# A gated delta mixer: transposed keys copied out of PSUM at once, decays fetched one head ahead

## Chip, cores and metric

The kernel runs on one core of one Trainium2 chip. The metric is the device time of one execution in microseconds. TensorE is written PE, VectorE DVE, ScalarE ACT, GpSimd POOL; SP is the engine whose queue issues the transfers.

## The reference

Two layers act on a sequence of 1024 tokens with 1024 features, all in float32. Each layer is a mixer, a cross-attention over 256 memory rows and a squared-ReLU MLP, each behind an RMS norm and added to the residual. The change lies in the mixer of the second layer, the gated delta rule with 8 heads of 128 x 128. Cut to what matters, it computes:

```
qkv, gate, b, a = split(h @ w_in)
qkv  = silu(short_conv(qkv, conv_w))           # 4 taps along the sequence
q, k = l2norm(q), l2norm(k)                    # per token and head, over 128 features
beta = sigmoid(b);  g = cumsum(-exp(a_log) * softplus(a + dt_bias))   # per chunk and head
decay[t, s] = exp(g[t] - g[s]) for s <= t, else 0
lower = beta * (k k^T) * decay (strict);  attn = (q k^T) * decay
u, w  = solve(1 + lower, [v * beta, k * beta * exp(g)])
per chunk:  v_new = u - w S;  o = (q exp(g)) S + attn v_new
            S = S exp(g_last) + (k exp(g_last - g))^T v_new
out = (rmsnorm(o) * silu(gate)) @ w_out
```

The kernel takes chunks of 128 tokens: eight chunks, four to a half of the sequence.

## The kernel before, in words

Activations are held with features on the 128 partitions and tokens along the free axis, in two halves of 512 tokens. Every large product is done three times with float32 split into a high and a low part (`mm3`). A projection of one head's 128 columns for one half is eight such triples, 24 products of 128x512 into one PSUM bank of tag "mm" (two banks).

`mix_c` runs the mixer. For each pair of heads it calls `gdn_head` twice, then `gdn_inv` (the triangular inverse, through DRAM) and `gdn_rec` (the recurrence over chunks; the last four heads run theirs together). Afterwards come eight gates (`c_gate`), whose projections depend on no head.

`gdn_head` projects keys, queries and values of a head (three weight tiles, both halves) into tiles "raw" (five buffers), and calls `gdn_pre` for each half. `gdn_pre` does this:

- conv and SiLU: one ACT multiply (L1002), three DVE multiply-adds (L1004), a tanh (L1007) and a DVE pass (L1008), for each of the three;
- keys are transposed by PE into a bank of tag "a" called pk (L1014). There are two such banks. ACT squares the four chunks from pk with a running sum (L1017) into `kt`, which serves as scratch here;
- the queries' squares are summed by PE into a second bank pn (L1022), which DVE copies out (L1023). From both sums come the norms, on DVE and with a power on POOL (L1024 to L1033);
- ACT scales the transposed keys, read from pk again, into `kt` (L1031), and `kt` is stored to DRAM;
- the decays M (128x512, the same row for all partitions) are fetched from DRAM into a tile of tag "M" with one buffer (L1037). ACT makes exp(M) for the queries (L1039), POOL multiplies it by the queries and subtracts the mask from M (L1040, L1042), and ACT makes the decay matrices in place (L1045);
- PE multiplies keys with keys and queries, two chunks to a bank of tag "a" (L1050), and DVE multiplies the result by norms and decays into `ua` (L1058), which is stored twice (L1066, L1088). Last, the values are transposed into a bank of tag "a" (L1071) and scaled (L1073).

`c_gate` projects the gate of a head, takes its SiLU (L881, L882), and for the heads 0 to 3 fetches the head's output from DRAM into the tile `e` (L884), multiplies (L885) and stores (L886).

Scratch of 128x512 comes from `tmp()`, tag "T" with five buffers: the conv's accumulators, the squares, the gate's `e`. Weight tiles go through `ldw` (two raw buffers, three split ones). All transfers are issued on SP, whose queue, like each engine's, runs in the order written. That order is fixed when the program is built: a planner goes through the instructions by priority (that of the program's text, unless marked high) and places each where its model of durations and free buffers says that it can start. An instruction whose input or buffer is late on the chip holds all that stand behind it on its engine.

Of the kernel before, what the change touches and what calls it, by code (L numbers as in the profile page):

```python
# [11 lines left out]
F32 = mybir.dt.float32  # L12
F32R = mybir.dt.float32r
BF16 = mybir.dt.bfloat16
AF = mybir.ActivationFunctionType
# [7 lines left out]
HALVES = (0, 1)  # L23
# [3 lines left out]
class Model:  # L27
# [336 lines left out]
    def mix(self, l):  # L364
        if l == 0:
            with self.phase(
                dict(z=3, so=1, ml=2),
                **dict(kq=8, v=4, e=2, sp=2, sh=2, sl=1, wh=2, wl=1, A=2, ah=1, al=1, so_st=1),
            ):
                self.mix_start(l, "so", dict(M=3, W=2, V=2, N=4, C=1, st=1, gg=1, ot=1))  # L370
                self.mix_ab()
                self.out_parts(False)
                self.x_open(self.x_src)
                self.out_proj(self.a["ab_o"])
        else:
            with self.phase(
                dict(a=2, i=1, rec=2, o=1),
                **dict(X=3, Y=2, Uk=1, pr=1, B=4, y=3, S=4, on=2),
            ):
                self.first = [self.ldw(self.a["c_w"][i]) for i in (8, 0)]  # L380
                self.mix_start(l, "o", dict(raw=5, kq=2, vc=1, M=1, qe=1, ua=1, kv=2))
                self.mix_c()
                self.out_parts(True)
                self.x_open(self.x_src, (1,))
                self.out_proj(self.a["c_o"])
# [214 lines left out]
    def ml_heads(self, p):  # L600
        nc = self.nc
        C = None
        for half in HALVES:
# [3 lines left out]
            for i in range(4):  # L607
# [3 lines left out]

                t = self.keep("M", 512, F32)
                qd, k, q = t[:, :256], t[:, 256:384], t[:, 384:]
                t = self.keep("M", 512, F32)
                vT, d = t[:, :256], t[:, 256:]
# [255 lines left out]
    def c_gate(self, h):  # L871

        nc = self.nc

        def gate(i, w, half):
            cols = slice(half * 512, half * 512 + 512)
            t, e = self.stage(), self.tmp()
            ps = self.proj(w, half)
            with self.tc.high_priority():
                self.scaled(t, ps, half)  # L880
            nc.scalar.activation(e, t, AF.Tanh, scale=0.5)  # L881
            nc.vector.scalar_tensor_tensor(out=t, in0=e, scalar=1.0, in1=t, op0=ALU.add, op1=ALU.mult)  # L882
            if h < 4:
                nc.sync.dma_start(out=e, in_=self.od[h][:, cols])  # L884
                nc.vector.tensor_mul(t, t, e)  # L885
            nc.sync.dma_start(out=self.pj[i][:, cols], in_=t)  # L886

        self.lagged([24 + h], lambda i: self.ldw(self.a["c_w"][i]), gate)
# [69 lines left out]
    def gdn_head(self, h):  # L958

        nc = self.nc  # L960
        raw = {}

        def take(i, w, half):
            t = self.ph2("raw", [128, 515])
            ps = self.proj(w, half)
            with self.tc.high_priority():
                self.scaled(t[:, 3:515], ps, half)
                if half == 0:
                    nc.gpsimd.memset(t[:, 0:3], 0.0)
                else:  # L970
                    nc.gpsimd.tensor_copy(t[:, 0:3], raw[i, 0][:, 512:515])
            raw[i, half] = t
            if (i, half) == (16, 0):
                self.c_gates()

        ld = lambda i: self.first.pop(0) if self.first else self.ldw(self.a["c_w"][i])
        self.lagged((8 + h, h, 16 + h), ld, take, 2 if h == 0 else 1)
        oq = self.cols([128, 8])
        for half in HALVES:
            self.gdn_pre(h, half, [raw[i, half] for i in (8 + h, h, 16 + h)], oq)  # L980
        return oq

    def ph2(self, tag, shape):
        pool = self.pr if tag in self.right else self.ph
        return pool.tile(list(shape), F32, tag=tag, name=self.nm(tag), bufs=self.bufs[tag])

    def gdn_pre(self, h, half, raws, oq):

        nc = self.nc
        mm = nc.tensor.matmul
        chunks = [slice(i * 128, i * 128 + 128) for i in range(4)]
        c4 = slice(4 * half, 4 * half + 4)
        kq = self.ph2("kq", [128, 2, 512])
        vc = self.keep("vc", dt=F32)
        for tl, raw, dst in zip((8 + h, h, 16 + h), raws, (kq[:, 0], kq[:, 1], vc)):
            cv = self.tmp()  # L1000
            wj = lambda j: self.convw[:, tl * 4 + j : tl * 4 + j + 1]
            nc.scalar.mul(cv, raw[:, 0:512], wj(0))  # L1002
            for j in range(1, 4):
                nc.vector.scalar_tensor_tensor(  # L1004
                    out=cv, in0=raw[:, j : j + 512], scalar=wj(j), in1=cv, op0=ALU.mult, op1=ALU.add
                )
            nc.scalar.activation(dst, cv, AF.Tanh, scale=0.5)  # L1007
            nc.vector.scalar_tensor_tensor(out=dst, in0=dst, scalar=1.0, in1=cv, op0=ALU.add, op1=ALU.mult)  # L1008
        self.put(h, half, 0, kq[:, 0])

        ss, r, c = (self.small([128, 8]) for _ in range(3))
        pk = self.bank("a")
        for s in chunks:
            nc.tensor.transpose(out=pk[:, s], in_=kq[:, 0, s], identity=self.ident)  # L1014
        kt = self.keep("kv", dt=F32)
        for i, s in enumerate(chunks):
            nc.scalar.activation(kt[:, s], pk[:, s], AF.Square, accum_out=ss[:, i : i + 1])  # L1017
        pn = self.bank("a")
        sq = self.tmp()
        nc.scalar.activation(sq, kq[:, 1], AF.Square)  # L1020
        for i, s in enumerate(chunks):
            mm(pn[:, i : i + 1], sq[:, s], self.ones[:, 0:1], start=True, stop=True)  # L1022
        nc.vector.tensor_copy(ss[:, 4:8], pn[:, 0:4])  # L1023
        nc.vector.tensor_scalar(out=ss, in0=ss, scalar1=0.25, scalar2=EPS, op0=ALU.mult, op1=ALU.add)  # L1024
        nc.gpsimd.tensor_tensor(out=r, in0=ss, in1=self.power, op=ALU.pow)
        nc.vector.reciprocal(c[:, 0:4], ss[:, 0:4])
        nc.vector.tensor_mul(c[:, 0:4], c[:, 0:4], self.gcol("beta", h, half))
        kd = c[:, 4:8]
        nc.vector.tensor_mul(kd, c[:, 0:4], self.gcol("ed", h, half))
        for i, s in enumerate(chunks):  # L1030
            nc.scalar.mul(kt[:, s], pk[:, s], kd[:, i : i + 1])  # L1031
        self.put(h, half, 3, kt)
        nc.vector.tensor_scalar_mul(oq[:, c4], r[:, 4:8], 0.5 * 128.0**-0.5)  # L1033

        M = self.keep("M", dt=F32)
        m3 = M.rearrange("p (c t) -> p c t", c=4)
        nc.sync.dma_start(out=m3, in_=self.gr[c4, h].partition_broadcast(128))  # L1037
        qe = self.keep("qe", dt=F32)
        nc.scalar.activation(qe, M, AF.Exp)  # L1039
        nc.gpsimd.tensor_mul(qe, qe, kq[:, 1])  # L1040
        self.put(h, half, 1, qe)
        nc.gpsimd.tensor_sub(m3, m3, self.mask_a.unsqueeze(1).broadcast_to([128, 4, 128]))  # L1042
        ng = self.gcol("ng", h, half)
        for i in range(4):
            nc.scalar.activation(m3[:, i], m3[:, i], AF.Exp, bias=ng[:, i : i + 1])  # L1045
        ua = self.ph2("ua", [128, 4, 2, 128])
        for i in range(0, 4, 2):
            p = self.bank("a")
            for j in range(2):
                mm(  # L1050
                    p[:, j * 256 : j * 256 + 256].rearrange("p (n t) -> p n t", n=2),
                    kq[:, 0, chunks[i + j]],
                    kq[:, :, chunks[i + j]],
                    start=True,
                    stop=True,
                )
            for j in range(2):
                nc.vector.scalar_tensor_tensor(  # L1058
                    out=ua[:, i + j],
                    in0=p[:, j * 256 : j * 256 + 256].rearrange("p (n t) -> p n t", n=2),  # L1060
                    scalar=c[:, i + j : i + j + 1],
                    in1=m3[:, i + j].unsqueeze(1).broadcast_to([128, 2, 128]),
                    op0=ALU.mult,
                    op1=ALU.mult,
                )
        nc.sync.dma_start(out=self.dense(self.Ud[h])[:, c4], in_=ua[:, :, 0])  # L1066
        self.put(h, half, 2, ua[:, :, 1])

        p = self.bank("a")
        for s in chunks:  # L1070
            nc.tensor.transpose(out=p[:, s], in_=vc[:, s], identity=self.ident)  # L1071
        t = self.keep("kv", dt=F32)
        nc.vector.tensor_mul(  # L1073
            t.rearrange("p (c d) -> p c d", c=4),
            p.rearrange("p (c d) -> p c d", c=4),
            r[:, 0:4].unsqueeze(2).broadcast_to([128, 4, 128]),
        )
        self.put(h, half, 4, t)
# [692 lines left out]
```

## Time and profile before

| | |
|---|---|
| runs | 3222.31, 3226.89, 3231.45 us; median 3226.89 |
| profiled execution | 3224.76 us, its span 3221.8 us |
| mean granted clock of PE | 0.971 of full speed |
| busy share of the span | PE 95%, PE's weight load 78%, DVE 66%, ACT 41%, POOL 29% |
| DMA | 438.04 MB, mean 136 GB/s |
| the chain that ended last | PE 33%, DVE 9%, DMA 4%, issue 4%, POOL 1%, ACT 1% |

The span runs from the first to the last instruction. Shares of busy time are means over stages that differ much. PE's clock has two levels, 1.2 and 2.4 GHz; a granted clock of 0.5 over a stretch means the lower level throughout.

### The profile page before, as it was taken

The numbers are of one execution on the slowest core, as the hardware profiler recorded it, in microseconds if no ns is written. First come the engines' busy times: TensorE is split into PE (matmuls) and PEld (weight loads), VectorE is DVE, ScalarE is ACT, GpSimd is POOL, SyncE is SP. The second block draws the span as 40 slices with busy tenths as digits, with TensorE's granted clock in tenths as the row PEclk, the third lists the DMA queues.
The fourth block names the chain that finished last, engine by engine and source line by source line (L and its number), as shares of the span: only waits on it lengthen the run. The fifth ranks groups of instructions, "written<-read, shape, count | busy, mean of one in ns | idle before, by whom it ended". The sixth has DMA issues, their size and how long they took to land.

```text
span 3221.8 us, 39997 instructions
## 1 busy us (share of the span) xinstructions
PE 3045.2 (95%) x14447; PEld 2511.5 (78%) x14447; DVE 2115.9 (66%) x3342; ACT 1330.2 (41%) x2525; POOL 945.4 (29%) x725
## 2 busy tenths in 40 slices
PE   8999989999899999998988899899999899999997
PEld 6777777888678878887777788788888678878886
DVE  5567475545786667777777775654454786667777
ACT  3254464424354454433443333234333354444442
POOL 2354565313000032234343333125323100023323
PEclk9999989999899999999999899999999999999998
DMA  4333553213244464443345556665212234474432
GB/s 151 109 119 103 156 175 119 70 39 102 75 143 157 152 238 167 147 164 100 87 117 142 149 156 187 191 231 187 66 56 77 97 111 149 157 250 173 148 144 79
DMA packets 268374, 438.04 MB, mean 136 GB/s; under 512 B 38064, under 2 KB 146832, under 8 KB 261008
## 3 DMA queue, kind: packets, MB, share of 16 engines
q1 hardware_dynamic: 268176, 435.50, 41.4%
q8 instruction: 113, 1.85, 0.2%
q14 instruction: 85, 0.70, 0.1%
HBM read 300.60 MB, written 134.81 MB: 135 GB/s over the span
## 4 chain that ended last, share of the span: by engine, by line
PE 33%; DVE 9%; DMA 4%; issue 4%; POOL 1%; ACT 1%; SPq 0%; POOLq 0%; DVEq 0%; ACTq 0%
PE mm L158 3%; PE mm L157 3%; PE mm L156 3%; PE ga L1453 2%; PE ga L1454 2%; PE ga L1455 2%; PE gb L1454 1%; DVE t L1004 1%; PE gb L1455 1%; PE gb L1453 1%; PE gc L1454 1%; PE gc L1455 1%; PE gc L1453 1%; PE mm L1454 1%; PE mm L1455 1%
## 5 line engine op out<-in xcount | busy, mean ns | idle before, releaser
L156 PE MATMUL mm<-hh,wh 128*128 128x512 f32 x1248 | 503.4, 404 | 8.2 <-DVE raw L431 3.5
L157 PE MATMUL mm<-hl,wh 128*128 128x512 f32 x1248 | 504.3, 404 | 0.0
L158 PE MATMUL mm<-hh,wl 128*128 128x512 f32 x1248 | 501.9, 402 | 0.0
L150 POOL TENSOR_TENSOR wl<-wr,wh 128x1024 fp32r<-128x1024 f32 x128 | 320.6, 2506 | 448.8 <-ACT wh L149 423.4
L1445 POOL TENSOR_TENSOR r<-r,r 128x512 f32<-128x512 f32 x64 | 92.0, 1458 | 881.8 <-DVE lo L1412 881.8
L1412 DVE TENSOR_TENSOR lo<-r,hi 128x1024 fp32r<-128x1024 f32 x192 | 252.8, 1317 | 133.1 <-ACT hi L1411 132.3
L1411 ACT CAST hi<-r 128x1024 fp32r<-128x1024 f32 x192 | 201.6, 1051 | 313.7 <-PE mm L1454 126.6
L156 PEld LDWEIGHTS mm<-hh,wh 128*128 128x128 f32 x1248 | 239.4, 192 | 59.2 <-DVE raw L431 4.8
L158 PEld LDWEIGHTS mm<-hh,wl 128*128 128x128 f32 x1248 | 240.5, 193 | 48.3 <-issue 0.9
L157 PEld LDWEIGHTS mm<-hl,wh 128*128 128x128 f32 x1248 | 240.2, 192 | 48.0 <-DVE hl L474 0.4
L149 ACT CAST wh<-wr 128x1024 fp32r<-128x1024 f32 x128 | 133.8, 1046 | 213.2 <-PE mm L157 120.8
L1412 DVE TENSOR_TENSOR lo<-br,hi 128x512 fp32r<-128x512 f32 x224 | 187.0, 852 | 32.9 <-ACT hi L1411 32.8
L1453 PE MATMUL ga<-hi,hi 128*128 128x512 f32 x528 | 206.7, 392 | 1.8 <-ACT w L1550 1.0
L1455 PE MATMUL ga<-hi,lo 128*128 128x512 f32 x528 | 206.5, 391 | 0.0
L1454 PE MATMUL ga<-lo,hi 128*128 128x512 f32 x528 | 206.5, 391 | 0.0
L1411 ACT CAST hi<-br 128x512 fp32r<-128x512 f32 x224 | 133.4, 619 | 152.0 <-PE ga L1455 90.0
L1454 PE MATMUL gb<-lo,hi 128*128 128x512 f32 x432 | 169.8, 393 | 7.6 <-DVE lo L1412 7.6
L1453 PE MATMUL gb<-hi,hi 128*128 128x512 f32 x432 | 169.8, 394 | 3.6 <-ACT hi L1411 3.1
L1454 PE MATMUL gc<-lo,hi 128*128 128x512 f32 x432 | 169.1, 391 | 2.3 <-DVE lo L1412 2.3
L1455 PE MATMUL gb<-hi,lo 128*128 128x512 f32 x432 | 169.0, 392 | 0.0
L1455 PE MATMUL gc<-hi,lo 128*128 128x512 f32 x432 | 168.2, 390 | 0.0
L1453 PE MATMUL gc<-hi,hi 128*128 128x512 f32 x432 | 167.8, 390 | 0.0
(515 smaller groups left out, 7228.5 us busy)
## 6 DMA issues: line engine op xcount, KB each, us to landing
r<-in_w SPq DMA_DIRECT2D x128, 512.0 KB, 4.2
br<-hd SPq DMA_DIRECT2D x56, 1024.0 KB, 5.4
hd<-w SPq DMA_DIRECT2D x160, 256.0 KB, 3.1
B<-Bd SPq DMA_DIRECT2D x64, 384.0 KB, 4.5
hd<-t SPq DMA_DIRECT2D x64, 256.0 KB, 5.2
wr<-in_c_w SPq DMA_DIRECT2D x32, 512.0 KB, 4.3
wr<-in_ab_w SPq DMA_DIRECT2D x24, 512.0 KB, 3.6
pj<-p SPq DMA_DIRECT2D x48, 256.0 KB, 2.1
```

The costliest lines, as they stand in the source:

```text
L149: nc.scalar.copy(hi, raw)
L150: (eng or nc.gpsimd).tensor_sub(lo, raw, hi.bitcast(F32))
L156: mm(out, w[0], x[0], start=first, stop=False)
L157: mm(out, w[0], x[1], start=False, stop=False)
L158: return mm(out, w[1], x[0], start=False, stop=last)
L1004: nc.vector.scalar_tensor_tensor(out=cv, in0=raw[:, j : j + 512], scalar=wj(j), in1=cv, op0=ALU.mult, op1=ALU.add)
L1411: nc.scalar.copy(hi, src)
L1412: (eng or nc.vector).tensor_sub(lo, src, hi.bitcast(F32))
L1445: self.nc.gpsimd.tensor_add(out[:, i : i + 512], a[:, i : i + 512], b[:, i : i + 512])
L1453: mm(ps, hi, b[k][0], start=first and k == 0, stop=False, skip_group_check=True)
L1454: mm(ps, hi, b[k][1], start=False, stop=False, skip_group_check=True)
L1455: mm(ps, lo, b[k][0], start=False, stop=last and k == 3, skip_group_check=True)
```

## The change

The scratch that the squares write is now a tile of its own; the transposed keys are copied to `kt` at once, and squares and scaling read `kt`. The fetch of M moves to a function `decays` that fetches both halves of a head; it is called before the head's projections, or for head 0 behind its gates, which make the rows that it reads. Tag "M" has two buffers in this phase. In the gate the fetch of the head's output goes into a tile `o` of its own, ahead of the projection.

```diff
-                self.mix_start(l, "o", dict(raw=5, kq=2, vc=1, M=1, qe=1, ua=1, kv=2))
+                self.mix_start(l, "o", dict(raw=5, kq=2, vc=1, M=2, qe=1, ua=1, kv=2))
...
             t, e = self.stage(), self.tmp()
+            if h < 4:
+                o = self.tmp()
+                nc.sync.dma_start(out=o, in_=self.od[h][:, cols])
             ps = self.proj(w, half)
...
             if h < 4:
-                nc.sync.dma_start(out=e, in_=self.od[h][:, cols])
-                nc.vector.tensor_mul(t, t, e)
+                nc.vector.tensor_mul(t, t, o)
             nc.sync.dma_start(out=self.pj[i][:, cols], in_=t)
...
         raw = {}
+        if h > 0:
+            M = self.decays(h)
...
         self.lagged((8 + h, h, 16 + h), ld, take, 2 if h == 0 else 1)
+        if h == 0:
+            M = self.decays(h)
         oq = self.cols([128, 8])
         for half in HALVES:
-            self.gdn_pre(h, half, [raw[i, half] for i in (8 + h, h, 16 + h)], oq)
+            self.gdn_pre(h, half, [raw[i, half] for i in (8 + h, h, 16 + h)], oq, M[half])
         return oq
+
+    def decays(self, h):
+
+        tiles = []
+        for half in HALVES:
+            tiles.append(self.keep("M", dt=F32))
+            self.nc.sync.dma_start(
+                out=tiles[half].rearrange("p (c t) -> p c t", c=4),
+                in_=self.gr[4 * half : 4 * half + 4, h].partition_broadcast(128),
+            )
+        return tiles
...
         kt = self.keep("kv", dt=F32)
+        nc.scalar.copy(kt, pk)
+        sq = self.tmp()
         for i, s in enumerate(chunks):
-            nc.scalar.activation(kt[:, s], pk[:, s], AF.Square, accum_out=ss[:, i : i + 1])
+            nc.scalar.activation(sq[:, s], kt[:, s], AF.Square, accum_out=ss[:, i : i + 1])
...
         for i, s in enumerate(chunks):
-            nc.scalar.mul(kt[:, s], pk[:, s], kd[:, i : i + 1])
+            nc.scalar.mul(kt[:, s], kt[:, s], kd[:, i : i + 1])
...
-        M = self.keep("M", dt=F32)
         m3 = M.rearrange("p (c t) -> p c t", c=4)
-        nc.sync.dma_start(out=m3, in_=self.gr[c4, h].partition_broadcast(128))
```

## Rows read from the trace of the kernel before

**Rows 1.** The page: span, and busy time of each engine.

```profile
span 3221.8 us, 39997 instructions
...
PE 3045.2 (95%) x14447; PEld 2511.5 (78%) x14447; DVE 2115.9 (66%) x3342; ACT 1330.2 (41%) x2525; POOL 945.4 (29%) x725
```

**Rows 2.** Windows: stretch, length, PE, PEld, DVE, ACT, POOL busy, clock, DMA share, GB/s.

```profile
1550.00:1730.00 180.00, 163.20 (x740) 131.22 (x738) 150.42 (x267) 76.74 (x200) 69.99 (x59) 0.96 0.41 111
1550.00:2130.00 580.00, 529.17 (x2808) 448.26 (x2807) 415.37 (x847) 210.70 (x560) 181.13 (x145) 0.95 0.53 152
```

**Rows 3.** Groups of PE, 1550:2130: busy, mean ns | idle before, releasers.

```profile
L156 PE MATMUL mm<-hh,wh 128*128 128x512 f32 x466 | 192.9, 414 | 2.8 <-DVE s L1027 2.3 <-DVE raw L431 0.5
...
L1050 PE MATMUL a<-kq 128*128 128x256 f32 x128 | 38.6, 429 | 13.0 <-DVE s L1023 6.6 <-ACT kv L1031 4.5 <-DVE ua L1058 2.0
...
L1071 PE MATMUL a<-ident,vc 128*128 128x128 f32 x64 | 10.5, 284 | 2.8 <-DVE ua L1058 2.8
...
L1014 PE MATMUL a<-ident,kq 128*128 128x128 f32 x64 | 9.8, 273 | 0.9 <-DVE ua L1058 0.9
```

**Rows 4.** Waits, 1540:2130: total us, times, longest.

```profile
ACT qe L1039 <- DMA M<-gr: 101.2, 16, 13.0
...
PE i L1129 <- DMA X<-Xd: 10.2, 4, 3.2
...
DVE p L885 <- DMA t<-od: 7.0, 6, 2.8
...
PE i L1129 <- DMA Uk<-Ud: 2.5, 1, 2.5
```

**Rows 5.** The line that fetches M: issue to landing.

```profile
DMA to landing us min/median/max: 4.7/6.8/8.8
```

**Rows 6.** Order of time, 1704:1717: start, length, instruction, [idle before].

```profile
1704.39 0.72 SPq L1037 DMA_DIRECT2D M<-gr  x1
...
1711.04 0.63 ACT L1039 ACTIVATE qe<-M 128x512 f32<-128x512 f32 x1 [3.43 <-DMA M<-gr]
...
1712.73 0.34 DVE L1024 TENSOR_SCALAR s<-s 128x8 f32<-128x8 f32 x1 [2.90 <-ACT kv L1017]
...
1716.22 0.47 PE L156 MATMUL mm<-hh,wh 128*128 128x512 f32 x1 [2.29 <-DVE s L1027]
```

**Rows 7.** Order of time, 1984:1990.

```profile
1984.52 0.63 ACT L1039 ACTIVATE qe<-M 128x512 f32<-128x512 f32 x1 [5.78 <-DMA M<-gr]
...
1987.01 0.49 PE L1190 MATMUL o<-S,B 128*128 128x128 f32 x2 [1.38 <-ACT on L1192]
...
1988.97 0.49 PE L1180 MATMUL rec<-y,B 128*128 128x128 f32 x2 [1.25 <-DVE y L1177]
```

**Rows 8.** Windows: stretches with a lower clock.

```profile
1595.00:1605.00 10.00, 7.70 (x27) 6.28 (x28) 9.32 (x15) 4.34 (x13) 7.06 (x6) 0.83 0.33 88
...
1715.00:1725.00 10.00, 8.37 (x32) 6.46 (x33) 9.79 (x29) 5.06 (x12) 4.47 (x5) 0.83 0.09 26
...
1985.00:2000.00 15.00, 12.37 (x68) 11.10 (x68) 7.47 (x17) 7.13 (x24) 5.96 (x4) 0.77 0.45 138
...
1730.00:1745.00 15.00, 11.84 (x53) 10.04 (x52) 8.37 (x17) 4.77 (x13) 5.22 (x5) 0.77 0.76 198
...
2085.00:2090.00 5.00, 5.00 (x23) 4.38 (x23) 1.68 (x3) 1.72 (x4) 0.00 (x0) 0.66 0.93 273
```

**Rows 9.** Single lines: min/median/max ns of one.

```profile
L1031 ACT ACTIVATE kv<-a,s x64: 347/367/381, 1575.7 to 1993.5; 128x128 f32<-128x128 f32 x64
...
L1045 ACT ACTIVATE M<-M,gd_ng x64: 384/387/416, 1562.4 to 1989.1; 128x128 f32<-128x128 f32 x64
...
L1550 ACT COPY w<-gb x28: 576/586/593, 896.4 to 2858.2; 128x512 f32<-128x512 f32 x28
```

**Rows 10.** SP's waits, 1540:2130.

```profile
SPq L1066 <- DVE ua L1058: 34.7, 8, 7.5
```

**Rows 11.** Order of time, PE at 2052.

```profile
2052.53 0.49 PE L1171 MATMUL rec<-S,B 128*128 128x128 f32 x2 [1.39 <-DVE S L1185]
```

More of the change, by code (lines that the diff above doesn't have):

```diff
@@ L985, in ph2, with gdn_pre @@
         return pool.tile(list(shape), F32, tag=tag, name=self.nm(tag), bufs=self.bufs[tag])
-    def gdn_pre(self, h, half, raws, oq):
+    def gdn_pre(self, h, half, raws, oq, M):
         nc = self.nc
```

## The prediction, made before the result was known

> **What bounds the kernel now.** I read the page's busy line first, then the second mixer in stretches, then who waits there, and last single stalls in order of time. TensorE (PE) is busy for 95% of the span [rows 1], so a microsecond counts only if PE stands idle in it or runs at a lower clock. The mixer's heads lie between 1550 and 2130 us. There PE is busy 529.17 of 580 us, so 50.8 us are idle, at a mean granted clock of 0.95. In the first 180 us of it VectorE (DVE) is busy 150.42 us, 84%: it is the second limit [rows 2].
>
> Which waits make up the idle time? The largest groups [rows 3]: the products of keys with keys and queries (L1050) wait 13.0 us, all for a bank of tag "a" (6.6 behind DVE's L1023, 4.5 behind ACT's scaling L1031, 2.0 behind L1058); the transposes L1071 and L1014 wait 2.8 and 0.9 us, for the same kind of bank behind L1058; a projection waits 2.3 us behind DVE's L1027; together 19.0 us. The inverse (L1129) waits 10.2 + 2.5 = 12.7 us for round trips through DRAM, and ACT, which is not the bound, waits 101.2 us in 16 waits for the decays M [rows 4]. That load takes 4.7 to 8.8 us to land [rows 5].
>
> That wait reaches PE. At 1704.39 M is issued, behind the stores of the previous half, since its one buffer is read until then. ACT's exponential of M starts at 1711.04 after 3.43 us of waiting, and the squares stand behind it on ACT. So DVE waits 2.90 us for their sum, and PE 2.29 us for a bank that DVE was to empty [rows 6]. The second example is another half: ACT waits 5.78 us for M, and behind it PE stops for 1.38 us (L1190) and 1.25 us (L1180) [rows 7].
>
> After such stops the clock falls. 1595:1605 was granted 0.83, which is 0.17 x 10 = 1.7 us lost. 1645:1650 and 1660:1670 lost 1.7 us each too, and 1715:1725 as well: four stretches, of which the first and the last are shown. 1985:2000, with 0.77, lost 3.45 us [rows 8].
>
> **The change part by part.**
>
> *Keys.* Today bank pk is held from the transposes through the squares, the sums, the power on GpSimd and the scaling L1031. Afterwards one copy frees it. Added are 16 copies of 128x512 out of PSUM; the same form (L1550) takes 586 ns at the median [rows 9], so 16 x 0.586 = 9.4 us of ACT. 128 short ACT operations now read SBUF. L1031 (PSUM, per-partition scale) has a median of 367 ns, L1045 (SBUF, per-partition bias) 387 ns. So 128 x 0.02 = 2.6 us. The other end is no difference, 0; as L1045 is also an exponential, the true price could even be under 0, which I bound by -2.6. I take 2.6, because L1045 is the nearest row with the same size and a scalar operand per partition too. The sum is 12.0 us on ACT, beside the 101.2 us that it waits today. If that cover were gone, ACT's lateness would reach PE at the rate at which it does now: 19.0 us of PE waits (below) against 101.2, or 0.19, so some 2.3 us. The squares also start 0.59 us later per half; this too is shorter than the wait that stood before them.
>
> The row says 20 ns more per short operation. The Trainium skill (Perfetto Trace Analysis, Optimizing Scalar/DVE Operations) speaks against the move: it states an access overhead of some 93 ns for ScalarE on SBUF against 51 ns on PSUM. By it the estimate would be 128 x 0.042 = 5.4 us instead of 2.6, and 14.8 us on ACT; the sum for PE would stay.
>
> What goes on PE: the 4.5 us behind L1031 (the second pair of L1050 needs pk's bank), and part of the 6.6 us behind L1023, since the first pair can take pk's bank instead of the one that L1023 empties. What is late next: both banks are now held by the two pairs until L1058, so L1071 and L1014 still wait for L1058. I therefore keep all waits behind L1058, 2.0 + 2.8 + 0.9 = 5.7 us, as not gained.
>
> *Decays.* The number of loads stays 16. With two buffers the load of a half waits for the same half of the head before, not for the half just done, so it is issued about half a head or more ahead, and a landing of 8.8 us at most is covered by the head's six projections: the row of L156 counts 466 products in the 580 us [rows 2, 3], eight to a projection, so 58 projections, one in 10 us on average. On SP's queue the load moves ahead of the weight loads, of the stores of keys and values, and of the loads of the inverse. All of these stand behind it if its buffer is not free. It waits for L1058, as the store L1066 already does for 34.7 us in 8 waits, at most 7.5 [rows 10]. A load that is queued after that store adds nothing; one queued before it holds weights for up to 7.5 us, which two weights in hand (three buffers, two projections each) cover. Only head 0 loads behind its own gates, as before. GpSimd's two passes over M move earlier but stay the same.
>
> *Gate.* For four heads the eight loads of earlier outputs go out before the projection, into a tile of their own. No load is added, but each holds one of the five "T" tiles through a projection. DVE waits 7.0 us for these loads today, in 6 waits [rows 4]; behind one of them PE stops 1.39 us at 2052.53 [rows 11]. I count 1.4. Bounds: 0 (the tile comes free late) and all of 7.0.
>
> *The sum.* PE waits 13.0 + 2.8 + 0.9 + 2.3 = 19.0 around the banks, 2.6 behind M at 1987 to 1989 [rows 7], 1.4 at the gate, and clock 4 x 1.7 + 3.45 = 10.25: together 33.3 us. Less the 5.7 behind L1058: 27.6 us. I count half. The order on each engine is fixed by a planner from modelled times, so the new order will have other places where PE comes too early; the profile can't show them, and half lies midway between "all gone" and "all replaced". That gives -13.8 us. The profiled execution took 3224.8 us (3221.8 of span and 3.0 around it), so 3211.0; the median of the three runs is 2.1 us above it: 3213 us.
>
> **The rivals.**
>
> 1. *Given back* (no change). M is no longer late, but PE's next limits are near: DVE at 84%, and the waits behind L1058. If only the 4.5 us behind L1031 and one clock fall of 1.7 go, the time is 3221. For it: DVE's load does not change by one instruction. Against it: DVE itself waits for ACT, as the 2.90 us show. That the change doesn't do what it says, because the loads are still issued late on SP, ends here too.
>
> 2. *All of it* (faster). Every counted stall goes, the ones behind L1058 as well, because M and the sums are both early: 3226.9 - 33.3 = 3194. For it: the waits in [rows 6, 7] have one root. Against it: with two banks of tag "a" something always waits for the second.
>
> 3. *The inverse comes out* (slower). The inverse's stores and loads through DRAM are covered by the work that PE does meanwhile. If the preparation of the heads runs through sooner, that work is used up sooner, and PE stands at L1129 more often. Five times today it waits there, 12.7 us in all [rows 4], and the stretches after have clocks of 0.77 (15 us), 0.66 (10), 0.66 (5), 0.66 (10) and 0.66 (5), of which the first and the last are shown [rows 8]: 3.45 + 3.4 + 1.7 + 3.4 + 1.7 = 13.65 us. One such stop costs 26.3 / 5 = 5.3 us. Doubling them costs 26.3, against 13.8 gained: 3239 us. It decides from about five more stops (26.5 - 13.8 = 12.7 us of loss, over 9.7), over four pairs of heads with two inverses each. For it: the loads there land later than PE comes even now. Against it: the gates' projections are free to fill, and an earlier preparation also starts the inverse earlier.
>
> **How the numbers follow.** The forecast (a gain of 7 to 20 us, 3207 to 3220) gets 0.42, rival 2 0.17, rival 1 0.25, rival 3 0.16. A measurement of this kernel tells a difference from none at about 0.3%, 9.7 us: faster is below 3217, slower above 3236. Of the forecast's 0.42 some 0.04 lies between 3217 and 3220; so faster is 0.38 + 0.17 = 0.55, same 0.25 + 0.04 = 0.29, slower 0.16. The range reaches from rival 2's 3194 to just beyond rival 3's 3239, so 3194 to 3240. The likeliest case alone would be 3207 to 3220.
>
> **What would show it.** The trace after should have ACT waiting for M under 20 us instead of 101.2; no PE wait behind L1031's successor; the copies at about 586 ns, the scalings within 20 ns of L1045's 387; waits of L1071 and L1014 about as now or a little more; PE idle in the mixer some 8 to 10 us less and the mean clock 0.96 or more. If ACT's wait goes and PE's idle time stays, rival 1 holds; if the waits at L1129 grow past 25 us, rival 3. The forecast would be wrong if M still arrives late, or if weight loads wait on SP behind it so that PE waits for weights, which it hardly does now.

## The result: slower by 0.65%, and what the profile after shows

The changed kernel took 3248.53 us (median of 4 runs, 3247.34 to 3251.64) beside 3226.52 us for the kernel before on the same chip. The ratio is 1.0065 (95% interval 1.0048 to 1.0081): slower by 0.65%. Forecast were 3213 us and a range of 3194 to 3240; the time lies outside it.

The page of the changed kernel: span, and busy time of each engine.

```profile
span 3247.9 us, 39980 instructions
...
PE 3053.5 (94%) x14447; PEld 2517.3 (78%) x14447; DVE 2112.6 (65%) x3342; ACT 1341.3 (41%) x2541; POOL 958.7 (30%) x725
```

Against [rows 1] the span is 26.1 us longer. PE has the same instructions and is busy 8.3 us longer, DVE 3.3 us less, and ACT 11.1 us longer. Where do the 26.1 us lie? The heads start at the same time in both (first convolution multiply at 1548.8 and 1548.4 us). The last step of the heads 0 to 3 gives a mark: the transposes of their finished outputs, L1212 before and L1229 after, eight to a head, with their first and last start. First the kernel before:

```profile
L1212 PE MATMUL o<-ident,on x32: 271/273/327, 1884.3 to 2081.3; 128*128 128x128 f32 x32
```

The same step after:

```profile
L1229 PE MATMUL o<-ident,on x32: 270/273/474, 1920.3 to 2106.8; 128*128 128x128 f32 x32
```

The last one starts 2106.8 - 2081.3 = 25.5 us later, the first even 36.0 us. So the loss lies in the second mixer's heads, and all of it is there by the time the outputs of the first two heads begin to be transposed. The same stretch in windows, the kernel before (columns as in [rows 2]):

```profile
1550.00:2160.00 610.00, 554.68 (x2981) 471.15 (x2980) 437.35 (x911) 230.76 (x627) 192.84 (x155) 0.95 0.55 159
```

and after, with its first 180 us:

```profile
1550.00:1730.00 180.00, 154.72 (x664) 126.06 (x663) 128.92 (x220) 68.11 (x169) 69.63 (x54) 0.90 0.38 103
1550.00:2160.00 610.00, 547.65 (x2905) 466.36 (x2904) 424.29 (x883) 230.50 (x618) 198.94 (x152) 0.92 0.53 151
```

In these 610 us PE stands idle 62.4 us instead of 55.3, and the granted clock is 0.92 instead of 0.95. The two don't add up to the loss in a simple way: a hundredth of the clock is 6.1 us here, and the changed kernel has got through less work in the same stretch (2905 instructions of PE against 2981). The whole span has the same 14447 instructions in both. There the 26.1 us are 17.8 us more idle time of PE (194.4 against 176.6) and 8.3 us more busy time. The mean granted clock of the span is 0.968 instead of 0.971, some 10 us in all, which fits the longer busy time. Look at DVE in the first 180 us: 128.92 us busy against 150.42 [rows 2]. DVE, the second limit, has as much to do as before and gets less done. Something keeps work from it.

Which PE waits? The groups of PE in 1550:2160 after, which answer to [rows 3]:

```profile
L156 PE MATMUL mm<-hh,wh 128*128 128x512 f32 x461 | 196.8, 427 | 15.4 <-DVE raw L431 14.4 <-DVE p L431 1.0
L1067 PE MATMUL a<-kq 128*128 128x256 f32 x128 | 44.7, 475 | 14.0 <-DVE s L1042 14.0
L1146 PE MATMUL i<-X,Uk 128*128 128x64 f32 x256 | 33.4, 280 | 5.0 <-issue 2.4 <-DMA X<-Xd 2.1 <-DVE B L1189 0.5
L1041 PE MATMUL a<-ones,t 128*128 128x1 f32 x128 | 17.7, 257 | 9.8 <-ACT t L1039 9.8
L1088 PE MATMUL a<-ident,vc 128*128 128x128 f32 x64 | 10.3, 272 | 0.0
L1031 PE MATMUL a<-ident,kq 128*128 128x128 f32 x64 | 10.3, 272 | 0.0
```

The 4.5 us behind the scaling, which the change was to remove, are gone. So are the waits of both transposes (2.8 and 0.9), which the prediction had kept. The inverse waits less, too. In their place PE waits 14.4 us with its projections, for a bank that DVE's L431 is to empty. It waits 14.0 us (6.6 before) behind DVE's copy of the sums, and 9.8 us for ACT's squares of the queries. All three stand behind work of ACT or DVE that comes late.

Waits of the changed kernel, 1540:2160: total us, times, longest.

```profile
ACT qe L1056 <- DMA M<-gr: 70.1, 14, 8.2
...
DVE t L1021 <- ACT t L1019: 50.5, 11, 7.6
...
DVE p L887 <- DMA t<-od: 3.6, 2, 2.5
```

ACT still waits 70.1 us for M (101.2 before, [rows 4]). DVE now waits 50.5 us for ACT's first multiply of a convolution; before it was 14.9 us:

```profile
DVE t L1004 <- ACT t L1002: 14.9, 13, 3.2
```

One half of the changed kernel in order of time shows how both come about:

```profile
1611.94 0.36 SPq L1083 DMA_DIRECT2D Ud<-ua  x1
...
1612.90 0.56 SPq L994 DMA_DIRECT2D M<-gr  x1
...
1615.45 0.68 DVE L1025 SCALAR_TENSOR_TENSOR vc<-vc,t 128x512 f32<-128x512 f32 x1
...
1620.18 0.63 ACT L1056 ACTIVATE qe<-M 128x512 f32<-128x512 f32 x1 [4.88 <-DMA M<-gr]
1620.72 0.57 ACT L1033 COPY kv<-a 128x512 f32<-128x512 f32 x1
1621.32 0.31 ACT L1036 ACTIVATE t<-kv 128x128 f32<-128x128 f32 x1
...
1622.51 0.62 ACT L1039 ACTIVATE t<-kq 128x512 f32<-128x512 f32 x1
1623.04 1.93 ACT L1019 ACTIVATE t<-raw,convw 128x512 f32<-128x512 f32 x3
...
1623.78 7.48 DVE L1021 SCALAR_TENSOR_TENSOR t<-raw,convw,t 128x512 f32<-128x512 f32 x8 [7.65 <-ACT t L1019]
1631.18 0.68 DVE L431 SCALAR_TENSOR_TENSOR raw<-mm,yy 128x512 f32<-128x512 f32 x1
...
1631.78 0.14 DVE L1042 COPY s<-a 128x4 f32<-128x4 f32 x1
...
1631.91 0.79 PE L156 MATMUL mm<-hh,wh 128*128 128x512 f32 x1 [4.06 <-DVE raw L431]
```

M's load is issued right behind the store L1083, which waits for the products that read the old M. The exponential of M starts at 1620.18 after waiting 4.88 us. Loads, exponentials and key copies each run in the order of the halves. Counted so, load and exponential are those of the fourth half, and the key copy at 1620.72 is that of the third: the exponential stands in front of the key copy of the half before it. Behind it on ACT stand the key copy, the squares of keys and queries, and then all three convolution multiplies of the next half in one piece. DVE, with nothing to do since 1616.1, has waited 7.65 us for them. Then it gets eight steps at once, 7.48 us, and the eviction L431 stands behind these. So PE, which has filled its projection banks meanwhile, stops for 4.06 us. DVE's copy of the sums (L1042) stands behind the eight steps as well.

Three causes offer themselves. Theory A: the squares' result now goes into a T tile (tag T, asked for by `self.tmp()`, five buffers), so that one half asks for five of the five T tiles, where it asked for four (three convolutions, the queries' squares). The planner may then find no tile for the next half's convolutions until it has placed the squares. Theory B: M's exponential stands too early in ACT's order, in front of the key copy, and everything behind it pays for the wait. Theory C: ACT simply has 12 us more to do.

### The profile page after: what moved, and what is told of

The parts are those of the page before. It is cut to its first block, busy times and chain, and to the rows that moved or that the text cites. A ratio compares the mean times of both kernels' runs of the same rounds, so it can differ in the third digit from the quotient of the medians.

```text
span 3247.9 us, 39980 instructions
## 1 busy us (share of the span) xinstructions
PE 3053.5 (94%) x14447; PEld 2517.3 (78%) x14447; DVE 2112.6 (65%) x3342; ACT 1341.3 (41%) x2541; POOL 958.7 (30%) x725
## 4 chain that ended last, share of the span: by engine, by line
PE 33%; DVE 9%; DMA 6%; issue 3%; ACT 2%; POOL 1%; SPq 0%; DVEq 0%; POOLq 0%; ACTq 0%
PE mm L156 3%; PE mm L157 3%; PE mm L158 3%; DVE t L1021 2%; PE ga L1470 2%; PE ga L1471 2%; PE ga L1472 2%; DMA M<-gr 2%; PE gb L1471 1%; PE gb L1470 1%; PE gb L1472 1%; PE gc L1471 1%; PE gc L1472 1%; PE gc L1470 1%; PE mm L1471 1%
```

## The experiments

All times are medians beside the kernel before on the same chip, which took 3224.6 to 3228.7 us in the five groups of runs; the ratio is to that.

**One edit at a time (e1_keys, e2_decays, e3_gate).** Each is the kernel before with one part of the diff. The first takes this part:

```
+        nc.scalar.copy(kt, pk)
+        sq = self.tmp()
...
-            nc.scalar.activation(kt[:, s], pk[:, s], AF.Square, ...)
+            nc.scalar.activation(sq[:, s], kt[:, s], AF.Square, ...)
...
-            nc.scalar.mul(kt[:, s], pk[:, s], kd[:, i : i + 1])
+            nc.scalar.mul(kt[:, s], kt[:, s], kd[:, i : i + 1])
```

Expected of the keys alone: 

> The kernel before with the keys edit alone (copy, squares into a tile of tag T, scaling from the copy); M still has one buffer and its old place. Theory A (the squares' result takes one of the five T tiles, so the three convolution multiplies of the next half can't be placed before this half's squares; DVE then starves at the convolutions): all or most of the 22 us, 3240 to 3250 us; DVE's wait for the convolution multiply (14.9 us in 13 before, 50.5 us in 11 after) is at 40 us or more. Theory B (the early load of M brings the exponential of the next half ahead of the key copy in ACT's order): 3227 within 7 us and DVE's wait as before, about 15 us. Theory C (ACT simply has 12 us more work and M's wait no longer covers it): 3229 to 3239.

Expected of the decays alone (M=2, and the loads in `decays`): 

> The kernel before with the decays edit alone (two buffers, loads ahead of the head's projections). Theory A: at or under the time before, 3217 to 3230 us, DVE's wait for the convolution multiply about 15 us. Theory B: 3240 to 3250 us, DVE's wait at 40 us or more, and ACT's wait for M (101.2 us before) at 70 us as in the kernel after.

Expected of the gate alone: 

> The kernel before with the gate edit alone (the earlier outputs are fetched ahead of the projection into a T tile of their own). Theories A and B: within 5 us of before (3222 to 3232), DVE's 7.0 us of waiting for these loads gone or halved. If A holds in a wider form (every added T tile costs, in the gates too), 3232 to 3240.

Measured: keys 3252.1 us, ratio 1.0071 (1.0045 to 1.0096); decays 3227.9, ratio 0.9997 (0.9984 to 1.0010); gate 3218.2, ratio 0.9975 (0.9959 to 0.9991). The keys edit alone makes the whole loss, with M as in the kernel before (2 us above what theory A gave). Its trace has the wait of DVE too:

```profile
DVE t L1004 <- ACT t L1002: 44.2, 11, 8.3
```

So theory B does not make the loss alone. The gate edit helps by 8 us, more than the 5 allowed for in the expectation.

**The tile by itself (before_sqt, before_sqown).** The keys edit is a copy, other operands and a tile. This run takes the tile alone into the kernel before:

```
+        sq = self.tmp()
         for i, s in enumerate(chunks):
-            nc.scalar.activation(kt[:, s], pk[:, s], AF.Square, ...)
+            nc.scalar.activation(sq[:, s], pk[:, s], AF.Square, ...)
```

> The kernel before with one thing added: the squares' result, which nobody reads, goes into a T tile instead of the key tile. No copy, the squares and the scaling read PSUM as before, no decays and no gate edit: no instruction more on any engine. Theory A (the T tile is the cost): 3243 to 3256 us, and the idle time of ACT's convolution multiply behind the projections (41.1 us before, 0.0 in the kernel with the keys edit alone) falls under 5 us, DVE's wait for it rises to 40 us or more. Rival (the copy and the SBUF operands are the cost, the tile only comes with them): 3221 to 3233 us.

Its counterpart has `sq = self.keep("qs", dt=F32)` in place of `self.tmp()`, with one buffer for the tag qs.

> The kernel before with the squares' result (which nobody reads) in a buffer of its own, the counterpart of the run in which it took a T tile (3264 us). Theory A: it is the tag that counts, so 3221 to 3234 us, as before, with ACT's convolution multiply again waiting some 30 to 45 us for the projections. If it were the place that is written (not the key tile), and not the T tile: 3255 to 3270 as with the T tile.

Measured: with the T tile 3264.5 us, ratio 1.0115 (1.0096 to 1.0133), with a tile of its own 3222.1, ratio 0.9997 (0.9984 to 1.0011). The two kernels have the same instructions on the same shapes; only the tag of one tile differs, and with it the loss goes from nothing to 1.2%, which is 8 us more than theory A had at most. Here is ACT in order of time, first with the T tile:

```profile
1623.90 0.63 ACT L1040 ACTIVATE qe<-M 128x512 f32<-128x512 f32 x1 [4.17 <-DMA M<-gr]
1624.44 0.26 ACT L1018 ACTIVATE t<-a 128x128 f32<-128x128 f32 x1
...
1625.44 0.64 ACT L1021 ACTIVATE t<-kq 128x512 f32<-128x512 f32 x1
1625.96 1.95 ACT L1002 ACTIVATE t<-raw,convw 128x512 f32<-128x512 f32 x3
```

then with a tile of its own:

```profile
1611.71 0.71 ACT L1002 ACTIVATE t<-raw,convw 128x512 f32<-128x512 f32 x1
1616.79 0.63 ACT L1040 ACTIVATE qe<-M 128x512 f32<-128x512 f32 x1 [4.37 <-DMA M<-gr]
1617.33 0.71 ACT L1002 ACTIVATE t<-raw,convw 128x512 f32<-128x512 f32 x1
1617.94 0.25 ACT L1018 ACTIVATE qs<-a 128x128 f32<-128x128 f32 x1
```

Both wait about as long for M. But with the tile of its own, one convolution multiply goes out ahead of the wait and a second ahead of the squares, so DVE has work during ACT's wait. With the T tile the three come as one piece, behind both squares. The groups of that line show it over all halves (busy, mean | idle before, releaser), with the T tile:

```profile
L1002 ACT ACTIVATE t<-raw,convw 128x512 f32<-128x512 f32 x48 | 31.2, 725 | 0.0
```

and with the tile of its own:

```profile
L1002 ACT ACTIVATE t<-raw,convw 128x512 f32<-128x512 f32 x48 | 34.0, 718 | 42.0 <-DVE raw L431 41.9
```

Idle time of 42.0 us before the multiply means that ACT got to it early and waited for the projection: it is as early as its data allow. Idle time of 0.0 means that it never waited for data; it was always late. That the T tile is the cost is shown, and the rival (copy and SBUF operands are the cost) is out. How it costs is shown only as far as the order on ACT. On the chip nobody waits for a tile: in the half of the changed kernel shown above, the last reader of the half's convolution tiles, L1025, ends at 1616.1, and the squares start at 1621.3, so that all five are free while ACT waits for M. What holds the multiplies back is their place in an order fixed beforehand. That the planner put them there because it counted no free tile is argued from the tag alone; no trace shows its books, and T with six buffers was not run.

Two signs set the five kernels with the squares in a T tile (the changed kernel, e1_keys, before_sqt and, below, after_held and after_m4) apart from the fourteen others. ACT is idle at most 6.7 us in all before the convolution multiplies, against 40 us or more. And PE waits 5.4 to 14.4 us for the bank that L431 empties, against 3.6 us at most. DVE's own wait for the multiplies is no such sign: it is 9.7 us in after_held, which is slow, and 31.1 us in own2_m4, which is fast.

**The changed kernel without the tile (own_sq, keys_own).** own_sq is the changed kernel with the squares in the tag qs; keys_own has the keys edit so, and nothing else.

> The changed kernel with all three edits, but the squares' result goes into a buffer of its own instead of a T tile. Theory A: the loss goes, 3215 to 3230 us, and DVE's wait for the convolution multiply falls from 50.5 us to 25 or less. Theory B: stays at 3244 to 3252, since M's exponential still stands in front. Theory C: 3240 or more, since ACT's work is the same.

> The kernel before with the keys edit alone and the squares in a buffer of their own; M keeps one buffer and its late load. Theory A with B' (a copy behind a late M): the keys edit is worth nothing as long as M is late, 3224 to 3240 us, with PE waiting 8 us or more for the copy. If early loads of M into two buffers were what brought the exponential ahead of the copy: 3210 to 3222 and no PE wait for the copy.

Measured: own_sq 3232.9 us, ratio 1.0020 (1.0007 to 1.0032); keys_own 3223.3, ratio 1.0001 (0.9989 to 1.0012). Without the T tile 14.5 us of the changed kernel's loss are gone (0.0045 x 3227); the median missed the first expectation's 3230 by 3 us. keys_own lies 1 us under its expectation and leaves no loss at all, so theory C is out: 12 us more of work on ACT cost nothing that can be measured. But three edits which cost nothing alone, or help, still lose 0.2% together. In own_sq PE waits for the new copy, longer than in keys_own (11.6 us in 8 waits):

```profile
PE a L1067 <- ACT kv L1033: 18.2, 8, 4.0
```

**What is left: M's exponential in front of the key copy (own_nogate, keys_own_gate, own_held, after_held).** own_nogate is own_sq without the gate edit; keys_own_gate is own_sq without the decays edit. own_held is own_sq with the exponential of M kept behind the scaling of its own half's keys, and after_held is the changed kernel with the same edit (`last` is the scaling's instruction):

```
+        with self.tc.issue_after(last.ins):
+            nc.scalar.activation(qe, M, AF.Exp)
```

> Keys edit with the squares in a buffer of their own, and M's two buffers, without the gate edit. With the gate edit it took 3232.9; without both, 3223.3. If M's two buffers and the keys edit hurt each other (theory B'): 3232 to 3244. If the gate's T tile and the keys edit hurt each other: 3220 to 3228.

> Keys edit with the squares in a buffer of their own, and the gate edit; M as in the kernel before. Theory B': the gains of the gate edit (0.25%) stay, 3212 to 3222. If the gate's T tile and the keys edit hurt each other: 3228 to 3238.

> The changed kernel with the squares in a buffer of their own (3232.9 us), two buffers for M, and the exponential of M held on ACT behind the scaling of its own half's keys, so that it no longer stands in front of that half's key copy. Theory B' (the copy behind the exponential's wait for M is what is left of the loss): 3208 to 3220 us, PE's wait for the copy under 9 us (18.2 before). Rival (the two-buffer loads cost elsewhere, or the gate's T tile does): 3226 to 3238 us.

> The changed kernel, squares in a T tile as they are, with the one edit that holds M's exponential behind the scaling of its own half's keys. Theory A: the T tile keeps most of the loss, 3236 to 3252. If the exponential in front of the key copy carried the loss: 3222 to 3232.

Measured: own_nogate 3235.5 us, ratio 1.0018 (1.0003 to 1.0034); keys_own_gate 3222.0, ratio 0.9979 (0.9963 to 0.9994); own_held 3204.4, ratio 0.9935 (0.9910 to 0.9960), 4 us better than expected; after_held 3248.3, ratio 1.0065 (1.0042 to 1.0087). It is the two M buffers and the keys edit that hurt each other, not the gate: the intervals of own_sq and keys_own_gate, which differ by the decays edit alone, do not touch (those of own_nogate and keys_own still do). The same place in own_sq:

```profile
1585.57 0.36 SPq L1083 DMA_DIRECT2D Ud<-ua  x1
...
1586.53 0.54 SPq L994 DMA_DIRECT2D M<-gr  x1
...
1593.31 0.63 ACT L1056 ACTIVATE qe<-M 128x512 f32<-128x512 f32 x1 [5.11 <-DMA M<-gr]
1593.84 0.57 ACT L1033 COPY kv<-a 128x512 f32<-128x512 f32 x1
...
1594.46 1.23 PE L1067 MATMUL a<-kq 128*128 128x256 f32 x4 [2.72 <-ACT kv L1033]
```

and in own_held:

```profile
1589.20 0.36 SPq L1084 DMA_DIRECT2D Ud<-ua  x1
...
1590.22 0.52 SPq L994 DMA_DIRECT2D M<-gr  x1
...
1592.36 0.59 ACT L1033 COPY kv<-a 128x512 f32<-128x512 f32 x1 [0.49 <-PE a L1031]
...
1603.97 0.62 ACT L1057 ACTIVATE qe<-M 128x512 f32<-128x512 f32 x1
...
1621.54 0.61 ACT L1057 ACTIVATE qe<-M 128x512 f32<-128x512 f32 x1
```

In both the load goes out 1 us behind the store of the half that held its buffer. In both it is the third load. In own_sq its exponential is next in ACT's order, and the copy, and with it PE, pays for the landing. In own_held the copy has waited for the transposes alone. The exponential at 1603.97 is the second; the third, which needs this load, comes at 1621.54, 31 us after its issue, and finds M landed. Its group there:

```profile
L1057 ACT ACTIVATE qe<-M 128x512 f32<-128x512 f32 x16 | 9.8, 615 | 0.0
```

No wait for M in 16 halves. The loads still go out right behind the half that held their buffer; it is the exponential that stands about half a head later. after_held separates the two causes: M's wait is gone there as well, and the loss stays. It differs from own_held by the T tile alone, which costs 42 us here (0.0130 x 3228). DVE no longer starves in front of the multiplies (9.7 us instead of 50.5). But in ten of the 16 halves they still come as one piece, and PE still stops behind it:

```profile
1611.72 1.93 ACT L1019 ACTIVATE t<-raw,convw 128x512 f32<-128x512 f32 x3
...
1618.04 0.68 DVE L431 SCALAR_TENSOR_TENSOR raw<-mm,yy 128x512 f32<-128x512 f32 x1
...
1618.78 0.50 PE L156 MATMUL mm<-hh,wh 128*128 128x512 f32 x1 [4.03 <-DVE raw L431]
```

**M really early (own_sq_m4, after_m4, gate_m4).** Four M buffers (`M=4`) let a load go out a head earlier. own_sq_m4 is own_sq so, after_m4 the changed kernel, gate_m4 the kernel before with the gate and decays edits.

> The changed kernel with the squares in a buffer of their own (3232.9 us) and four buffers for M instead of two, so that a load waits for nothing of the head just done. Theory B' (what is left of the loss is the key copy, which stands on ACT behind the exponential that waits for M: the products of keys wait for the copy 18.2 us of PE in 8 waits): 3210 to 3224 us, the wait for M under 20 us, the wait for the copy under 6. Rival C' (what is left is ACT's own 12 us of work, or the planner's other order): 3228 to 3238, though M's wait goes.

> The changed kernel with one size changed: four buffers for M; the squares stay in a T tile. It shows how much of the loss is left when M is early but the T tile is missing. Theory A: ACT's convolution multiplies still stand in a lump, 3230 to 3248 us, DVE's wait for them 30 us or more. If the late M was as much the cause as the T tile: 3215 to 3228.

> The kernel before with the gate edit and early loads of M into four buffers; keys as before. If the late M costs the kernel what the prediction counted (2.6 us of PE waits, and about half of the clock's 10 us), 3204 to 3214 us and ACT's wait for M under 20 us; if M's wait is free on ACT, 3215 to 3222 as with the gate edit alone (3218.2).

Measured: own_sq_m4 3210.0 us, ratio 0.9939 (0.9920 to 0.9958); after_m4 3225.9, ratio 1.0002 (0.9991 to 1.0013); gate_m4 3216.1, ratio 0.9960 (0.9946 to 0.9974). In own_sq_m4 ACT's wait for M is down to one of 6.8 us, and the wait for the copy from 18.2 to 4.7 us. gate_m4, where the wait for M is down to 7.8 us, is not told apart from the gate edit alone: as long as the keys stay as they were, M's wait on ACT is nearly free. after_m4 missed what theory A expected, in time and in DVE's wait (22.4 us): the early M gave back 0.63% although the squares still took a T tile. The two causes do not add. The tile costs 20 us with M early (0.0063 between own_sq_m4 and after_m4), 14.5 with M late (own_sq and the changed kernel) and the 42 us above with the exponential held. Why removing the wait by a load that lands sooner frees after_m4, and removing it by order does not free after_held, is open; after_held waits 15.2 us at the inverse (L1147) and after_m4 7.3, but no run tells what sets that.

**Still fewer T tiles (gate_qs, own2_m4).** If one tile too few hurts, does one more help? Here the queries' squares leave the T tiles too, in the gate edit alone and in own_sq_m4.

> The kernel before with the gate edit, and the squares of the queries moved out of the T tiles into a buffer of their own: one tile held less where the changed kernel held one more. Theory A in its full form (each T tile in the preparation of a half sets how far ahead the convolutions run): 3203 to 3215 us. If five tiles already sufficed, so that only the sixth demand hurts: 3215 to 3222, as with the gate edit alone.

> The version that beats both so far (3210.0 us: three edits, the squares in a buffer of their own, four buffers for M) with the squares of the queries out of the T tiles too (two buffers for squares). If T tiles are still short: 3195 to 3207. If five without the key squares suffice: 3206 to 3214, no difference.

Measured: gate_qs 3215.3 us, ratio 0.9962 (0.9949 to 0.9975), own2_m4 3212.0, ratio 0.9952 (0.9935 to 0.9969); 3218.2 and 3210.0 without. No difference that these runs can tell: where a half took four of the five tiles, three gained nothing, while five of five cost 14.5 to 42 us. In the range tried it is a threshold, not a slope.

**The best version (own_held_m4).** Both remedies for M, the squares in their own tile, and the gate edit.

> Both remedies for the late M at once: the exponential of M held behind the scaling of its own half's keys (alone 3204.4 us) and four buffers for M (alone 3210.0 us); the squares in a buffer of their own. If both cure the same thing, the exponential in front of the key copy: 3200 to 3212, no further gain. If M was late even behind the scaling, or the order and the load are two costs: 3188 to 3198.

Measured: 3199.3 us, ratio 0.9917 (0.9905 to 0.9930), faster than both kernels. Against own_held alone it is 0.0018 better, which is within that run's interval; the time fell between the two expectations, so that most of the two remedies is one cost. Its mixer in windows:

```profile
1550.00:2160.00 610.00, 571.81 (x3223) 496.38 (x3222) 451.34 (x952) 257.85 (x690) 211.40 (x165) 0.96 0.58 170
```

PE is idle 38.2 us there, 17.1 less than in the same stretch of the kernel before. So the gain that the prediction wanted was there to be had, with a few lines more.

## Why the prediction was wrong, point by point

*The step that failed.* "Keys" counted what ACT would do and which bank would come free. It did not count the buffer that the new line takes: `sq = self.tmp()`, a fifth T tile per half. So the cost of that line was put at nothing without a reason. The prediction named the five T tiles under "Gate", where one is held through a projection, and that use proved harmless (the gate alone gained). Under "Keys", where the tile made the half's demand five of five, it named none. The runs put 1.2% on that tag alone (before_sqt against before_sqown), 0.7% in the keys edit (e1_keys against keys_own), and 14.5 of the 21 us in the changed kernel (own_sq); the rest is the step under "Decays". The sign of the forecast fell with it. The prediction expected new single stalls; what came was another order in the halves, with the convolution multiplies late throughout (ACT idle 0.0 us before all 48 of them).

*The size of the keys edit* was nearly right. Medians of the single lines after, to be set beside [rows 9]:

```profile
L1033 ACT COPY kv<-a x16: 565/570/589, 1568.8 to 2001.3; 128x512 f32<-128x512 f32 x16
...
L1050 ACT ACTIVATE kv<-kv,s x64: 384/387/407, 1582.5 to 2010.7; 128x128 f32<-128x128 f32 x64
```

The copy took 570 ns where 586 was counted, the scaling 387 against 367, which is just the 20 ns taken from L1045. The squares with their accumulator rows took 30.9 us instead of 29.7, so 9.2 + 2.5 + 1.2 = 12.9 us against 12.0 forecast. The estimate by the overheads that the Trainium skill states (Perfetto Trace Analysis, Optimizing Scalar/DVE Operations) was 14.8 us; the trace is nearer to the rows. "The cover" held: keys_own does this work at a ratio of 1.0001.

*What goes on PE.* The 4.5 us behind the scaling went, as said. Of the 6.6 us behind DVE's copy of the sums a part was to go as well; they grew to 14.0. In the half shown above the copy (L1042, 1631.78) stands on DVE behind the eight convolution steps and the eviction, so this too goes with the multiplies' coming late. The waits of L1071 and L1014, kept as not gained, went after all.

*Decays.* "Issued about half a head or more ahead" came true, and its consequence, that the landing is covered, failed. As predicted, the load waits for the products of the same half a head earlier; it stands on SP right behind their store, at 1612.90 in the example. The key copy of the load's own half comes 35 us later:

```profile
1648.30 0.57 ACT L1033 COPY kv<-a 128x512 f32<-128x512 f32 x1
```

But the exponential did not stay beside it. In ACT's new order it follows the load at once, at 1620.18, half a head ahead of its own keys. The forecast was an ACT wait under 20 us; it was 70.1. Rival 1 covers the decays alone in its outcome, no difference in time, but not in its reason ("the loads are still issued late on SP"). What no rival had is that an exponential moved up in ACT's order by a load that the planner takes to be early makes the key copy wait. The prediction had put the copy behind that wait as something shorter than it, and so free. In own_sq it cost PE 18.2 us, and own_held, without it, gained 0.85% on own_sq.

*Gate.* 1.4 us were counted with bounds of 0 and 7.0; the edit alone gave 8 us (0.0025 x 3228, interval 3 to 13). DVE's wait for the outputs fell from 7.0 to 1.6 us in that run. In 1550:2160 PE was idle 48.4 us instead of 55.3 (610 less 561.61 and 554.68 busy), about the upper bound by itself, and the clock was 0.96 instead of 0.95. The clock was in the sum, but not under this edit. What else the gate edit set free, no run takes apart.

*Rival 3*, the slower side, put the loss at the inverse. It did not come: 5.0 us at L1146, of 12.7 before. So the side had a chance of 0.16, but from a mechanism that did not occur, and the range ended at 3240, where that mechanism ended.

*Half of what was counted* was justified by "the new order will have other places where PE comes too early". This was the right worry. It should have been bounded from the other side as well: an order that is worse in every half, not only one that gives half of the gain back.

## What to carry to other kernels

Before a line's price is worked out, list every buffer that it takes, with the tag's count and how many one turn of the loop already holds: here a half that took all five had the next half's work come late, and that alone cost 1.2%. A load moved up is early only if its buffer is free early and its reader does not move up with it, so look at what its issue waits for and at what reads it (7 us after the issue in the changed kernel, 31 us in own_held); and whatever the engine does behind the instruction that needs it waits as well. Idle time before an instruction that nothing else needs yet can be a good sign: 42.0 us before the convolution multiply meant that it was early, 0.0 that it was late.

## What the runs showed that was not expected

- A 128x128 square with its accumulator read costs nearly the same from either memory: from PSUM 272 ns and 205 for the accumulator, from SBUF 297 and 187 (means over 64). The slower read of the source is mostly given back in the accumulator's row.
- About a third of this loss is longer busy time at a lower clock: of the 26.1 us, PE's idle time is 17.8, and its same 14447 instructions take 8.3 us more. One stop of 2.9 to 5.5 us in each half went with it: in 1550:1730, where six such stops stand and PE is busy 154.72 of 180 us, the granted clock was 0.90, against 0.96 before with 163.20 busy.
